# Placing the rows of matmul operands within 512 bytes in an encoder block on one Trainium2 core

## Chip, core and metric

The kernel runs on one core of one Trainium2 chip. The metric is the device time of one execution in microseconds (us). A difference between two kernels counts as one from about 0.5%.

## What is computed

One residual block for a stream of 2048 tokens of width 1024, in float32:

```
n  = rms_norm(x);  q|k|v|u|B|C|gate_attn|gate_conv = n @ W_in + b_in
A  = chunked attention, 8 heads of 64, each chunk of 64 sees itself and 8 before it
yB = B * dwconv3_causal(C * u)
h  = x + (sigmoid(gate_attn) * (A @ P_attn) + sigmoid(gate_conv) * (yB @ P_conv)) @ W_o
h += moe(rms_norm(h))            # 32 experts, 2 per token, w2(silu(x w1) * (x w3))
out = h + sigmoid(rms_norm(h) @ W_pg + b_pg) * (p @ W_pp)
```

## The kernel before

Nearly all the work is matmuls on TensorE. Every float32 operand is split into two parts, `hi` (a rounded copy, made by ScalarE, L79) and `lo` (the rest, a subtraction on VectorE or GpSimd, L80), and a product is made in three passes that add up in PSUM (`mm3`, L82 to L93: L90 hi x hi, L91, L92). In `matmul(ps, stationary, moving)` the stationary operand has 128 columns of 4 bytes, one row of 512 bytes per partition, and the moving one mostly 512 columns, 2048 bytes per partition. In the profile's names a matmul is written `acc<-moving,stationary`.

The stages follow each other, with some overlap:

- Stage 1 (to about 640 us): q, k, v of each tile of 128 tokens (`proj`: moving `wh`, `wl`; stationary `nh`, `nl`), scores (`KT` moving, `QT` stationary, L346), transposes of the probabilities (L378) and their product with the values (L391, L392).
- Stage 2 (to about 1650 us), in four blocks of 512 tokens: `conv` (three products of 24 matmuls for each of four groups of channels) and `gate` (two products of 24 matmuls, and then `proj_T(ch, ya)` and `proj_T(ch, yc, 4)` of 12 each, for each of eight groups) have the token operands `nh`, `nl`, `yh`, `yl`, `ych`, `ycl` moving and the weight chunks `whi`, `wlo` stationary; `out_proj` has the chunks moving and `mh`, `ml` stationary. Routing (L668 to L760) runs between them, and near its end the first halves of p @ W_pp (`plain`: `wpph`, `wppl` moving, `ph`, `pl` stationary).
- Stage 3 (to about 2465 us): 32 experts in an order by their token counts; 18 of them have room for 192 tokens (rows A of 128 and B of 64), the others for 128. `gemm1` multiplies `xAh`, `xAl` and `xB` (stationary) with chunks of w1 and w3, `gemm2` `aAh`, `aAl` and `aB` with chunks of w2. B is one stationary of hi and lo side by side, so it needs two passes (L1034, L1035).
- Stage 4: the last gate, `whi`, `wlo` and one resident chunk `w7h`, `w7l` moving, `xh`, `xl` stationary.

The weights come as a stream of chunks of 512 KB (`prefetch`, L451 to L466): SP's queue loads `wraw` (L458), the split makes `whi` and `wlo`, 7 buffers of each in stages 3 and 4, 4 in stage 2, and TensorE frees them.

The addresses of the tiles follow from the order and the sizes in which the pools hand them out: pools of the left side (`cst`, `s1att`, `s2left`, `s3two`, `s4two`) grow upwards, pools of `side="right"` (`keep`, `wstream`, `s2right`, `ppool`) downwards. A tile of an odd size moves all that come behind it.

Of the kernel before, what the change touches and what calls it, by code (L numbers as in the profile page):

```python
# [7 lines left out]
F32 = mybir.dt.float32  # L8
# [7 lines left out]
DRAM = bass.MemoryType.DRAM  # L16
# [8 lines left out]
NE = 32  # L25
CAP = 192
NBIG = 18
# [18 lines left out]
def triangle():  # L46
    """[p < j | 1]"""
    return np.concatenate([np.arange(128)[:, None] < np.arange(128)[None, :], np.ones((128, 128))], 1).astype(np.float32)


def constants():
    c = np.zeros((128, NCST), np.float32)
    put = lambda n, v: c.__setitem__((slice(None), slice(*CO[n])), v)
    put("iota", np.arange(CAP))
    put("i4", 4 - np.arange(4))
    put("i8", 8 - np.arange(8))
    put("p", np.arange(128)[:, None])
    # expert 0 comes first whatever its count
    key = NE - 1 - np.arange(NE) + (np.arange(NE) == 0) * 2.0 ** 20
    put("key", key)  # L60
    put("kcol", key[np.arange(128) % NE][:, None])
    put("eid", (np.arange(128) % NE)[:, None])
    return c


# relative position of query row i of a tile and key column j of its band of 640
# [7 lines left out]
class K:  # L74
# [7 lines left out]
    def mm3(self, ps, st, mv, i0, n):  # L82
        """ps += st.T @ mv in three passes; st, mv = lists of (hi, lo)"""
        k = len(st)
        for i in range(k):
            sh, sl = st[i]
            mh, ml = mv[i]
            first = (i0 + i == 0)
            last = (i0 + i == n - 1)
            self.nc.tensor.matmul(ps, sh, mh, start=first, stop=False)  # L90
            self.nc.tensor.matmul(ps, sh, ml, start=False, stop=False)  # L91
            mm = self.nc.tensor.matmul(ps, sl, mh, start=False, stop=last)  # L92
        return mm  # L93

    # ---------------------------------------------------------------- setup
# [17 lines left out]

    def bank(self, dt=F32):
        self.nbank += 1
        return self.banks[self.nbank % len(self.banks)].tile([128, 512], dt, name="acc")

    def rstd(self, out, ss, n, width=1):
        """out = (ss/n + eps) ** -0.5 on Pool"""
        nc = self.nc  # L120
        nc.gpsimd.tensor_scalar(out, ss, 1.0 / n, EPS, op0=ALU.mult, op1=ALU.add)
        return nc.gpsimd.tensor_tensor(out, out, self.mhalf[:, :width], op=ALU.pow)

    # ---------------------------------------------------------------- stage 1
    def stage1(self, outer, after, lead=11, lag=2):
        tc, nc, a = self.tc, self.nc, self.a
        with ExitStack() as ctx:
# [14 lines left out]
            # the places of what the attention needs later serve the first loads  # L142
# [49 lines left out]
            # ---- projections of one tile, in four pieces  # L192
# [134 lines left out]
            # ---- attention, a unit = one head of one query tile  # L327
# [80 lines left out]
            fill = None  # L408
# [23 lines left out]
    # ---------------------------------------------------------------- weights, as a stream of [128, 1024] chunks  # L432
    def open_keep(self, ctx):
        nc = self.nc
        self.cst = ctx.enter_context(self.tc.tile_pool(name="keep", bufs=1, side="right", reuse_waits="tile"))
        self.cs = self.cst.tile([128, NCST], F32, name="cs")
        nc.scalar.dma_start(self.cs, self.a["cst"])
        self.gple = self.cst.tile([128, 8], F32, name="gple")
        nc.scalar.dma_start(self.gple, self.a["g_ple"][0].rearrange("(k p) -> p k", p=128))
# [7 lines left out]
    def add_chunk(self, parts, lo_eng=None, scale=None):  # L447
        """parts: function that gives [(view of a raw [128, 1024] tile, DRAM AP)]"""
        self.wsrc.append((parts, lo_eng, scale))
# [15 lines left out]
    def split_scaled(self, raw, hi, lo, scale, eng=None):  # L465
        """hi + lo = raw, or raw * scale with scale [128, 1]"""  # L466
        nc = self.nc
        if scale is None:
            return self.split(raw, hi, lo, lo_eng=eng)
        nc.scalar.activation(hi, raw, AF.Copy, scale=scale)  # L470
        nc.vector.scalar_tensor_tensor(lo, raw, scale, hi.bitcast(F32), op0=ALU.mult, op1=ALU.subtract)

    def chunk(self, ahead=2):
        """hi and lo of the next chunk; issues the chunks up to that one + ahead"""
        i = self.wcur
        self.wcur += 1
        self.prefetch(i + ahead)
        return self.wdone.pop(i)

    # ---------------------------------------------------------------- stage 2  # L480
    def stage2(self, outer, inner):
        """a generator: what it gives before the attention is done needs only the right side and ps_acc"""
# [18 lines left out]
        # what routing keeps  # L501
# [10 lines left out]
        with ExitStack() as ctx:  # L512
# [4 lines left out]
            bT = one([128, 28], "bT")  # L517
            nc.scalar.dma_start(bT, a["b_in"][0, 1536:5120].rearrange("(c p) -> p c", p=128))
            cw = one([128, 3, 4], "cw")
            for j in range(3):  # L520
                nc.scalar.dma_start(cw[:, j], a["conv_w"][0, j].rearrange("(c p) -> p c", p=128))
            cb = one([128, 4], "cb")
# [4 lines left out]
            halo = one([128, 4, 2], "halo")  # L527
# [24 lines left out]
            def proj_T(ch, n, k0=0):  # L552
                """[128 channels, 512 tokens]"""
                ps = bank()
                K_ = len(n)
                st = [(ch[0][:, (k0 + k) * 128:(k0 + k + 1) * 128], ch[1][:, (k0 + k) * 128:(k0 + k + 1) * 128]) for k in range(K_)]
                self.mm3(ps, st, n, 0, K_)
                return ps

            def conv(b, c, n):  # L560
# [5 lines left out]
                z = rt.tile([128, 514], F32, name="z", bufs=1)  # L566
# [34 lines left out]
            def out_proj(b, m):  # L601
                """a generator of the four tiles of block b"""
# [42 lines left out]
            def tail1(b, j, h):  # L645
                """h and its norm to DRAM; the norm's factor"""
                t0 = 512 * b + 128 * j
                nc.sync.dma_start(self.H[t0:t0 + 128, :], h)
                n2 = two.tile([128, D], F32, name="n2", bufs=2)
                ss = two.tile([128, 1], F32, name="ss")  # L650
                self.squared = nc.scalar.activation(n2, h, AF.Square, accum_out=ss)
                r = two.tile([128, 1], F32, name="rr", bufs=4)
                self.rooted = self.rstd(r, ss, D)
                nc.vector.scalar_tensor_tensor(n2, h, r, gffn, op0=ALU.mult, op1=ALU.mult)
                nc.sync.dma_start(self.N2[t0:t0 + 128, :], n2)
                return h, r

            def tail2(j, hr, LG):
                """the router's logits of the normed rows: (h * g @ w) * r + b"""
# [13 lines left out]
            def route(b, LG):  # L673
                """a generator: up to the ranks' matmuls, up to the slots' matmuls, the rest"""
# [64 lines left out]
                pick = T("pick", [4, NE])  # L739
# [22 lines left out]
            # from here on the left side is free too  # L762
# [4 lines left out]
            gT = two.tile([128, 8, 1], F32, name="gT", bufs=1)  # L767
            nc.scalar.dma_start(gT[:, :, 0], a["g_ffn"][0].rearrange("(k p) -> p k", p=128))
            wr = two.tile([128, 8, 36], F32, name="wr", bufs=1)
# [3 lines left out]
            br = two.tile([128, 36], F32, name="br", bufs=1)  # L773
# [48 lines left out]
    # ---------------------------------------------------------------- experts in the order of their counts  # L822
    def sort(self, pool, bank):
        """position of each expert by its count (0 for expert 0); the tokens of each position, the rows their outputs go to"""
# [16 lines left out]
        # pm[(q, e), i] = (pos[e] == i) * (1 or 128)  # L841
# [20 lines left out]
        # a slot that no token fills writes a row that nobody reads  # L862
        cT = T("cT", [32, 128])
# [5 lines left out]
        # blocks of 128 that the experts' tokens past their room fill  # L869
# [22 lines left out]
    def overflow_rows(self, pool):  # L892
        """for the tokens past their expert's room: place in the blocks of 128 that follow; the expert of each block"""
# [29 lines left out]
        # expert of block i = number of ends <= i  # L923
# [27 lines left out]
    # ---------------------------------------------------------------- stage 3  # L951
    def stage3(self):
# [3 lines left out]
        # positions below NBIG have room for CAP tokens, the others for 128; the two kinds alternate  # L956
# [31 lines left out]
        with ExitStack() as ctx:  # L988
# [48 lines left out]
            def fold(out, ps):  # L1037
                """out = the two halves of a B product, added"""
# [4 lines left out]
            def gemm1(x, gb=None):  # L1043
                """with gb the first matrix meets the rows A, then the rows B"""
# [192 lines left out]
    # ---------------------------------------------------------------- p @ w_ple_proj  # L1237
# [11 lines left out]
    def pp_half(self, n):  # L1249
        """the next n halves of tiles of p @ w_ple_proj, to DRAM, behind the last marked matmul"""  # L1250
# [21 lines left out]
    def plain(self, t, pool, name, bufs, eng=None):  # L1272
        """128 rows of p @ w_ple_proj, a generator of its halves"""
# [14 lines left out]
    # ---------------------------------------------------------------- stage 4  # L1288
    def stage4(self, out):
        tc, nc, a = self.tc, self.nc, self.a  # L1290
        with ExitStack() as ctx:
# [57 lines left out]
            def finish(t, h, r, pgs, pp, cuts, last):  # L1349
                """h + sigmoid(h * g @ w * r + b) * pp"""  # L1350
# [22 lines left out]
            order.close()  # L1373
            add(todo[0], *ld[0][:2])
            xs = turn(ld[0][1])
            r = norm(*ld[0][:2])
            for i, t in enumerate(todo):
# [8 lines left out]
                # the last tile's second half comes in two parts, each stored when it is done  # L1386
# [53 lines left out]
```

## Time and profile before

| what | value |
|---|---|
| time of three runs | 2697.61, 2699.0, 2709.66 us (median 2699.0) |
| span of the profiled execution, first to last instruction | 2698.6 us (the profile gives no other time of it) |
| TensorE matmul busy | 2636.4 us, 98% |
| VectorE, ScalarE, GpSimd busy | 62%, 50%, 31% |
| bytes from and to HBM | 400.30 and 62.39 MB, 171 GB/s over the span |

A busy share is a mean over stages. Matmuls overlap in this profile, so the time that one takes from the stream is the distance between two starts, not the duration of one.

### The profile page before, as it was taken

Reading aid. Unit: us, or ns where it says so; the run is one execution under the profiler, and the core shown is the slowest. Engines: PE = TensorE matmul, PEld = TensorE weight load, DVE = VectorE, ACT = ScalarE, POOL = GpSimd, SP = SyncE. Lnnn points to the kernel's source line nnn. Section 1 sums busy time; section 2 is a strip of 40 time slices with the busy share of each in tenths; the row PEclk is TensorE's granted clock in tenths of the full one; section 3 lists DMA queues with packets and bytes.
Section 4 is the critical chain, followed back from the end, with each engine's and each line's share of the span. In section 5 each row is a group of like instructions: output and inputs, shape, how many; then the busy total and the mean of one; then the engine's idle time right before and its main releaser. Section 6 shows DMA issues by size and latency. Waiting matters only on the chain.

```text
span 2698.6 us, 36516 instructions
## 1 busy us (share of the span) xinstructions
PE 2636.4 (98%) x13313; PEld 2183.9 (81%) x13313; DVE 1672.3 (62%) x2399; ACT 1341.7 (50%) x2025; POOL 838.2 (31%) x681
## 2 busy tenths in 40 slices
PE   7999999999999999999999998999999999998999
PEld 6888888878888888888888886888888888887887
DVE  7788867775344444444545446677777778675654
ACT  5666665563233323332333224766666666665322
POOL 2665565510000100010001003544544545452222
PEclk9999999999999999999999998999999999999999
DMA  5221311054345334533453346888988889887653
GB/s 182 71 71 56 109 47 40 9 137 139 95 139 172 102 94 141 172 94 94 142 162 94 94 149 211 302 303 289 308 302 302 294 295 314 301 301 264 215 180 109
DMA packets 349624, 465.11 MB, mean 172 GB/s; under 512 B 26241, under 2 KB 222081, under 8 KB 349441
## 3 DMA queue, kind: packets, MB, share of 16 engines
q1 hardware_dynamic: 314944, 388.35, 44.3%
q0 software_dynamic: 12096, 43.00, 4.4%
q10 hardware_dynamic: 22400, 31.41, 3.5%
q8 instruction: 105, 1.72, 0.3%
q14 instruction: 79, 0.64, 0.1%
HBM read 400.30 MB, written 62.39 MB: 171 GB/s over the span
## 4 chain that ended last, share of the span: by engine, by line
PE 89%; DVE 5%; DMA 2%; issue 1%; ACT 1%; POOL 1%; another core or an unknown queue 0%; ACTq 0%; SPq 0%; DVEq 0%; POOLq 0%
PE acc L90 24%; PE acc L92 23%; PE acc L91 23%; PE acc L1034 4%; PE acc L1035 4%; PE big L346 2%; PE big L378 2%; PE acc L391 1%; PE acc L392 1%; PE acc L1003 1%; PE acc L670 1%; DMA wraw<-w 1%; PE acc L292 1%; DVE PTl L384 1%; PE acc L1084 0%
## 5 line engine op out<-in xcount | busy, mean ns | idle before, releaser
L80 DVE TENSOR_TENSOR wlo<-wraw,whi 128x1024 fp32r<-128x1024 f32 x464 | 690.4, 1499 | 506.8 <-ACT whi L79 495.4
L79 ACT CAST whi<-wraw 128x1024 fp32r<-128x1024 f32 x560 | 584.9, 1050 | 810.5 <-PE acc L91 388.5
L90 PE MATMUL acc<-nh,whi 128*128 128x512 f32 x896 | 355.1, 398 | 1.0 <-ACT nh L79 1.0
L91 PE MATMUL acc<-nl,whi 128*128 128x512 f32 x896 | 355.2, 396 | 0.0
L92 PE MATMUL acc<-nh,wlo 128*128 128x512 f32 x896 | 354.3, 395 | 0.0
L80 POOL TENSOR_TENSOR wlo<-wraw,whi 128x1024 fp32r<-128x1024 f32 x96 | 236.5, 2464 | 130.8 <-ACT whi L79 122.1
L595 POOL TENSOR_TENSOR sa<-sa,sc 128x512 f32<-128x512 f32 x32 | 41.4, 1294 | 553.2 <-DVE sc L594 506.9
L90 PE MATMUL acc<-whi,xAh 128*128 128x512 f32 x512 | 207.1, 404 | 0.0
L91 PE MATMUL acc<-wlo,xAh 128*128 128x512 f32 x512 | 203.0, 397 | 0.0
L92 PE MATMUL acc<-whi,xAl 128*128 128x512 f32 x512 | 202.9, 397 | 0.0
L90 PEld LDWEIGHTS acc<-nh,whi 128*128 128x128 f32 x896 | 168.2, 188 | 41.2 <-ACT nh L79 1.9
L92 PEld LDWEIGHTS acc<-nh,wlo 128*128 128x128 f32 x896 | 168.4, 188 | 39.8
L91 PEld LDWEIGHTS acc<-nl,whi 128*128 128x128 f32 x896 | 168.5, 188 | 38.5
L91 PE MATMUL acc<-wl,nh 128*128 128x256 f32 (+1 forms) x512 | 173.8, 340 | 3.3 <-DVE wl L80 3.3
L90 PE MATMUL acc<-wh,nh 128*128 128x512 f32 (+1 forms) x512 | 175.9, 344 | 0.0
L92 PE MATMUL acc<-wh,nl 128*128 128x256 f32 (+1 forms) x512 | 174.3, 341 | 0.0
L383 ACT CAST PTh<-big 128x640 fp32r<-128x640 f32 (+4 forms) x128 | 80.3, 628 | 83.8 <-PE big L378 82.8
L365 ACT ACTIVATE L<-L,mn 128x640 f32<-128x640 f32 (+4 forms) x128 | 98.4, 769 | 38.6 <-DVE mn L363 15.1
L92 PEld LDWEIGHTS acc<-whi,xAl 128*128 128x128 f32 x512 | 96.6, 189 | 23.6 <-DVE xAl L1007 0.2
L90 PEld LDWEIGHTS acc<-whi,xAh 128*128 128x128 f32 x512 | 96.7, 189 | 22.7 <-ACT xAh L1006 0.2
L1034 PE MATMUL acc<-whi,xB 128*128 128x512 f32 x288 | 114.5, 398 | 0.0
L91 PEld LDWEIGHTS acc<-wlo,xAh 128*128 128x128 f32 x512 | 96.9, 189 | 21.5
(328 smaller groups left out, 5944.1 us busy)
## 6 DMA issues: line engine op xcount, KB each, us to landing
wraw<-w SPq DMA_DIRECT2D x384, 512.0 KB
wraw<-w_in SPq DMA_DIRECT2D x112, 512.0 KB
wraw<-w_o SPq DMA_DIRECT2D x32, 512.0 KB
y<-Y SPq DMA_DIRECT2D x32, 512.0 KB
xt<-x SPq DMA_DIRECT2D x16, 512.0 KB
xt<-NTd SPq DMA_DIRECT2D x16, 512.0 KB
nraw<-NTd ACTq DMA_DIRECT2D x32, 256.0 KB
wraw<-w_pa SPq DMA_DIRECT2D x32, 256.0 KB
```

The lines of the kernel that those rows point to most:

```text
L79: (hi_eng or self.nc.scalar.copy)(hi, raw)
L80: (lo_eng or self.nc.vector).tensor_sub(lo, raw, hi.bitcast(F32))
L90: self.nc.tensor.matmul(ps, sh, mh, start=first, stop=False)
L91: self.nc.tensor.matmul(ps, sh, ml, start=False, stop=False)
L92: mm = self.nc.tensor.matmul(ps, sl, mh, start=False, stop=last)
L346: nc.tensor.matmul(big[:, 512 * c:512 * c + hi - lo], QT[g, t][:, s, h * 128:(h + 1) * 128], KT[0][:, h, ks:ks + hi - lo], start=(s == 0), ...
L365: nc.scalar.activation(L[:, :n], L[:, :n], AF.Exp, bias=mn, scale=-1.0, accum_out=sm)
L378: nc.tensor.transpose(pt[:, j * 128:(j + 1) * 128], L[:, j * 128:(j + 1) * 128], self.ident)
L383: nc.scalar.copy(hi, ptv)
L595: nc.gpsimd.tensor_tensor(sa, sa, sc, op=ALU.add)
L1034: nc.tensor.matmul(ps, st, ch[0][:, sl], start=first, stop=False)
L1035: nc.tensor.matmul(ps, st, ch[1][:, sl], start=False, stop=last)
```

## The change

It gives tiles of other sizes, so that what follows them lies elsewhere; it adds three tiles that nobody uses (`pad`), puts several small tiles in one (`small`, `misc`), and lets two small tiles take the place of others of the same size (`pick` that of `prod`, `cT` that of `rk`). The core of the diff (removed comments left out):

```diff
 def setup(self, ctx):
         self.banks, self.nbank = [], 0
+        c.tile([128, 88], F32, name="pad")
...
 def open_keep(self, ctx):
         nc.scalar.dma_start(self.cs, self.a["cst"])
+        self.cst.tile([128, 24], F32, name="pad")
...
 def stage2(self, outer, inner):
-            bT = one([128, 28], "bT")
+            small = one([128, 128], "small")
+            bT = small[:, 0:28]
-            cw = one([128, 3, 4], "cw")
+            cw = small[:, 28:40].rearrange("p (j c) -> p j c", j=3)
-            cb = one([128, 4], "cb")
+            cb = small[:, 40:44]
-            halo = one([128, 4, 2], "halo")
+            halo = small[:, 44:52].rearrange("p (c j) -> p c j", j=2)
...
-                z = rt.tile([128, 514], F32, name="z", bufs=1)
+                z = rt.tile([128, 640], F32, name="z", bufs=1)
...
-                pick = T("pick", [4, NE])
+                pick = T("prod", [4, NE])
...
-            gT = two.tile([128, 8, 1], F32, name="gT", bufs=1)
+            misc = two.tile([128, 448], F32, name="misc", bufs=1)
+            gT = misc[:, 0:8, None]
-            wr = two.tile([128, 8, 36], F32, name="wr", bufs=1)
+            wr = misc[:, 8:296].rearrange("p (k c) -> p k c", k=8)
-            br = two.tile([128, 36], F32, name="br", bufs=1)
+            br = misc[:, 296:332]
...
 def sort(self, pool, bank):
-        cT = T("cT", [32, 128])
+        cT = T("rk", [32, 128])
...
 def stage4(self, out):
             order.close()
+            two.tile([128, 48], F32, name="pad", bufs=1)
```

Every engine has the same instructions in the same order, but for the copy `cT` of `sort`, which VectorE now runs behind one small subtraction and not ahead of it. No wait is added. What changes is where operands begin. The table gives the first byte of each operand within a row of 512 bytes of its partition, and the distance from the moving rows to the stationary rows, modulo 512, both as the addresses of the two built programs have them:

```
matmuls                       before: moving, stationary, distance   after
stage 1  wh,wl / nh,nl        288  288    0                          288  288    0
         KT / QT              160 or 416  160   0 or 256             0 or 256  0   0 or 256
         PTh,PTl / Vt         160  160    0                            0    0    0
stage 2  nh,nl / whi,wlo       64   96   32                            0    0    0
         yh,yl / whi,wlo      480   96  128                          256    0  256
         ych,ycl / whi,wlo     96   96    0                            0    0    0
         whi,wlo / mh,ml       96  480  384                            0  256  256
         wpph,wppl / ph,pl     96   96    0                            0    0    0
stage 3  whi,wlo / xA,xB       96  160   64                            0    0    0
         whi,wlo / aA,aB       96  160   64                            0    0    0
stage 4  whi,wlo / xh,xl       96  160   64                            0  192  192
         w7h,w7l / xh,xl      160  160    0                            0  192  192
```

## Rows read from the trace of the kernel before

**Rows 1.** The page's first part: busy us (share of the span) x instructions.

```profile
PE 2636.4 (98%) x13313; PEld 2183.9 (81%) x13313; DVE 1672.3 (62%) x2399; ACT 1341.7 (50%) x2025; POOL 838.2 (31%) x681
```

**Rows 2.** The page's chain that ended last, shares of the span by engine.

```profile
PE 89%; DVE 5%; DMA 2%; issue 1%; ACT 1%; POOL 1%; another core or an unknown queue 0%; ACTq 0%; SPq 0%; DVEq 0%; POOLq 0%
```

**Rows 3.** Busy time in a stretch of stage 2 and one of stage 3.

```profile
core 0: us, PE busy (x) PEld busy (x) DVE busy (x) ACT busy (x) POOL busy (x), PEclk, DMA share, GB/s
1000.00:1300.00 300.00, 300.00 (x1358) 243.85 (x1357) 139.48 (x189) 102.34 (x130) 22.50 (x28) 1.00 0.39 123
1660.00:2340.00 680.00, 680.00 (x3185) 547.55 (x3184) 494.65 (x466) 448.71 (x561) 334.64 (x179) 1.00 0.87 297
```

**Rows 4.** Timeline, stage 2: start us, us, engine, line, operation, out<-moving,stationary; PEld loads weights.

```profile
1100.08 0.40 PE L90 MATMUL acc<-nh,whi 128*128 128x512 f32 x1
1100.08 0.19 PEld L91 LDWEIGHTS acc<-nl,whi 128*128 128x128 f32 x1
...
1100.31 0.40 PE L91 MATMUL acc<-nl,whi 128*128 128x512 f32 x1
```

**Rows 5.** Timeline of PE, stage 2: first and last of 48 matmuls, distance 32.

```profile
1089.59 0.40 PE L90 MATMUL acc<-nh,whi 128*128 128x512 f32 x1
...
1100.55 0.39 PE L92 MATMUL acc<-nh,wlo 128*128 128x512 f32 x1
```

**Rows 6.** Timeline of PE, stage 3: first and last of 65 matmuls, distance 64.

```profile
1781.65 0.40 PE L90 MATMUL acc<-whi,xAh 128*128 128x512 f32 x1
...
1796.58 0.39 PE L1035 MATMUL acc<-wlo,xB 128*128 128x512 f32 x1
```

**Rows 7.** Timeline of PE, stage 2, out_proj: first and last of 192 matmuls, distance 384.

```profile
787.21 0.40 PE L90 MATMUL acc<-whi,mh 128*128 128x512 f32 x1
...
831.60 0.40 PE L92 MATMUL acc<-whi,ml 128*128 128x512 f32 x1
```

**Rows 8.** Timeline of PE, one gate: 12 of y, 12 of yc, then nh.

```profile
681.17 0.39 PE L90 MATMUL acc<-yh,whi 128*128 128x512 f32 x1
...
683.98 0.39 PE L90 MATMUL acc<-ych,whi 128*128 128x512 f32 x1
...
685.36 0.39 PE L90 MATMUL acc<-ych,whi 128*128 128x512 f32 x1
...
686.72 0.40 PE L90 MATMUL acc<-nh,whi 128*128 128x512 f32 x1
```

**Rows 9.** Timeline of PE, p @ w: two of 24 matmuls at distance 0, 11 steps apart.

```profile
1620.90 0.39 PE L90 MATMUL acc<-wpph,ph 128*128 128x512 f32 x1
...
1623.39 0.39 PE L92 MATMUL acc<-wpph,pl 128*128 128x512 f32 x1
```

**Rows 10.** Groups of matmuls, forms apart: xcount | busy us, mean ns | idle before.

```profile
L90 PE MATMUL acc<-nh,whi 128*128 128x512 f32 x896 | 355.1, 398 | 1.0 <-ACT nh L79 1.0
...
L90 PE MATMUL acc<-whi,xAh 128*128 128x512 f32 x512 | 207.1, 404 | 0.0
...
L90 PE MATMUL acc<-whi,mh 128*128 128x512 f32 x256 | 101.3, 396 | 0.0
...
L90 PE MATMUL acc<-whi,xh 128*128 128x512 f32 x217 | 86.8, 401 | 0.4 <-ACT xh L1336 0.4
...
L90 PE MATMUL acc<-ych,whi 128*128 128x512 f32 x128 | 50.1, 392 | 0.0
...
L90 PE MATMUL acc<-w7h,xh 128*128 128x512 f32 x31 | 12.1, 389 | 0.0
```

**Rows 11.** Timeline of PE, stage 1: four score matmuls (one row), and what follows.

```profile
611.70 0.75 PE L346 MATMUL big<-KT,QT 128*128 128x320 f32 x4
612.29 0.28 PE L391 MATMUL acc<-PTh,Vt 128*128 128x256 f32 x1
```

**Rows 12.** The page's costliest groups: the split on DVE.

```profile
L80 DVE TENSOR_TENSOR wlo<-wraw,whi 128x1024 fp32r<-128x1024 f32 x464 | 690.4, 1499 | 506.8 <-ACT whi L79 495.4
```

**Rows 13.** Waits of SP's queue, the longest: us in total, times, longest us.

```profile
SPq L458 <- DVE wlo L80: 1100.2, 390, 7.6
```

## The prediction

> **What bounds the kernel now.** I read the page first, then the chain of waits, then busy time by stretches, then the forms of matmul, and last the timeline of TensorE (PE), where the change acts. PE is busy for 2636.4 of 2698.6 us [rows 1] and carries 89% of the chain that ended last [rows 2]; in the long stretches of stages 2 and 3 it is never idle (300 of 300 us, 680 of 680 us) at a granted clock of 1.00, the 2.4 GHz level [rows 3]. A change of a few ns for each matmul is therefore a change of the end, as long as operands keep arriving.
>
> How far apart two matmuls start is not the printed duration: with starts 0.23 us apart each row shows 0.40 us, because the matmuls overlap. I use differences of starts ("pitch") over long runs, so that the rounding to 0.01 us does no harm. 512 columns at 2.4 GHz are 213.3 ns. Beside each matmul the weight load of the next one runs: L91's load starts at 1100.08, with the matmul of L90, and its own matmul at 1100.31 [rows 4]. So the pair that reads on-chip memory (SBUF) at one time is the moving rows of one matmul and the stationary rows of the next, and their distance is what the change sets.
>
> The pitches by distance within a row of 512 bytes (table of the section on the change) are these:
> - distance 32 (nh, whi): 47 steps from 1089.59 to 1100.55, 233.2 ns [rows 5];
> - distance 64 (whi, xA): 64 steps from 1781.65 to 1796.58, 233.3 ns [rows 6];
> - distance 384 (whi, mh): 191 steps from 787.21 to 831.60, 232.4 ns [rows 7];
> - distance 128 (yh, whi): 12 steps from 681.17 to 683.98, 234.2 ns; and right behind it, same stage, same moving form, same whi, distance 0 (ych, whi): 12 steps to 686.72, 228.3 ns, of which the first six take 230.0 and the last six (from 685.36) 226.7 [rows 8];
> - distance 0 again (wpph, ph): 11 steps from 1620.90 to 1623.39, 226.4 ns [rows 9].
>
> So distance 0 settles some six matmuls after a disturbance at about 226.7 ns, 13.3 above the 213.3 of streaming; the others stay at 233.3, 20 above. That step of 6.6 ns is what the sum is made of. The mean durations agree: 398 for nh and 404 for xA, 392 for ych, 389 for w7h [rows 10].
>
> **The change, part by part.** No engine gets another instruction or another wait; the order stays, but for one DVE copy (below). Only addresses move. I take 227.0 ns for a matmul at distance 0 after the change: 226.7, and some 20 ns more (six matmuls at 230.0) after each break, spread over runs of 48 to 80.
>
> 1. Stage 2, nh and nl with whi and wlo, 32 to 0: 2688 matmuls (896 on each of three lines [rows 10]) x (233.2 - 227.0) = 16.7 us.
> 2. Stage 2, y with whi, 128 to 256, and yc with whi, which stays at 0 but begins at byte 0: 32 gate steps, each now 2.81 + 2.74 us [rows 8], then 24 x 0.227 = 5.45, so 0.10 each, 3.2 us. Distance 256 has one witness: four score matmuls of 320 columns start at 611.70 and the next form at 612.29, 147.5 ns each, 14 above their 133.3 [rows 11]; their moving rows begin at 160 and at 416 in turn, against 160, so half of them stand at 256 and all are as cheap as 0. Bounds: 128's price kept (0.5 us left, from yc) and that of 0 (3.2). I take the latter.
> 3. Stage 2, whi with m, 384 to 256: 768 matmuls (256 on each line [rows 10]) x (232.4 - 227.0) = 4.1 us; bounds 0 and 4.1, by the same witness.
> 4. Stage 3, whi with xA, xB, aA, aB, 64 to 0: xA 3 x 512 [rows 10]; the code gives 32 experts x 8 x 3 = 768 for aA, 18 x 16 x 2 = 576 for xB, 18 x 8 x 2 = 288 for aB; 3168 in all x 6.3 = 20.0 us.
> 5. Stage 4, whi with xh and xl, 64 to 192: 3 x 217 = 651 matmuls [rows 10]. No row shows 192. It lies between 128 (no gain) and 256 (6.3 ns, 4.1 us): I take the middle, 2.1 us. The 3 x 31 of w7 leave 0 for 192; now 389 where xh has 401 [rows 10], so the bounds are nothing and 93 x 6.3 = 0.6 us lost. I take nothing, since they never run more than three in a row.
> 6. At nothing: the score and P.V matmuls (distances stay 0 and 256), the projections of stage 1 (288 on both sides stays), transposes, the wider z, the scalars gathered in two tiles, and the shared names. The copy cT falls behind one small subtract on DVE while PE has other halves of p @ w to do; with that cover gone it costs less than the 1.5 us of a full split [rows 12].
>
> Sum: 16.7 + 3.2 + 4.1 + 20.0 + 2.1 = 46.1 us. The profiled execution's span is 2698.6; the page gives no time around it, and the median of the three runs is 2699.0, 0.4 more. I predict 2699.0 - 46.1, rounded to **2653 us**.
>
> Does all of it reach the end? Stage 3 is the place to ask: DMA's share is 0.87 at 297 GB/s [rows 3], and a pitch 2.7% shorter asks for about 0.89 and 305. But the queue that loads weights waits for buffers, not they for it: 390 waits on DVE's split, 1100.2 us in all [rows 13], and the split waits for buffers that PE frees. A faster PE shortens these waits first. Late next would be the weights of the experts with room for 128 tokens, which have the fewest matmuls for the same bytes, with a few us.
>
> **A rule that speaks against this.** The forecast stands on rows 5 to 9 alone. The Trainium skill (TensorE: Matmul & The Clock Gate, "Step-by-step: what each phase is for") says that PE has two independent SBUF read ports, one for the moving operand and one for the weight load, so that loading the next weights steals nothing from the running matmul. By that the sum would be 0 and the time 2699; by the rows it is 46. Rows 8 disagree with it: two kinds of run follow each other in one stage, alike in form, and differ by 6 to 7 ns a matmul.
>
> **The rivals.**
> - *It seldom settles.* Transposes and changes of operand break the runs, and the mean stays at 229.5 to 230, as in the first six of ych [rows 8]. Gain 3.5 ns x 7659 matmuls (the sum of 1 and 3 to 5, with 384 for y) = 27 us: **2672**. For it: many runs of 12 in stage 2. Against: most are 48 to 80 long, and neighbours get the same distance.
> - *A start at byte 0 gives a further step.* All distances that I can read are of rows that begin inside a row of 512. Moving rows of 2048 bytes that begin at 0 touch four such rows and not five. If that is worth one more step of 6.7 ns for the 8136 matmuls concerned (7659, and 477 of yc and w7), the gain is 46 + 54: **2599**. Nothing in the trace shows it; only that steps of this size exist speaks for it.
> - *Nothing changes* because distance is not the cause, but the place of a run or its operands: **2699**. Against it: 0 is cheap at two starting bytes (96 and 160), in two stages [rows 8 to 10].
> - *Slower.* With both rows at byte 0, weight load and matmul, which start together [rows 4], meet at the first byte, and each matmul pays one step more than today: 8136 x 6.7 = 54 us, **2753**. It decides from a mean pitch of 235 (1.7 ns above today's 233.3, 13.5 us in all). For it: no moving row of 512 columns begins at 0 today. Against: the pairs at 96 (yc, ph) meet at their first byte too, and are the cheapest.
>
> **How the numbers follow.** Forecast 0.62 (by itself 2640 to 2665, from the bounds of 2, 3 and 5 and a few us for late loads), seldom settles 0.13, a further step 0.12, nothing 0.08, slower 0.05. Leaving out the last two leaves out 0.13, so the range goes from just below the third case to just above the first rival: 2597 to 2684. About 0.5%, 13.5 us, is what a measurement here can tell from no change: the first three cases are faster by more (0.87), the fourth is within it (0.08), the last slower (0.05).
>
> **What would show it.** Right: runs of nh, xA and mh at 226.7 ns, their mean durations down from 396 to 404 to about 390; stage 3 some 20 us and stage 2 some 24 us shorter, stage 1 as it is; PE still never idle there. Wrong: runs of xA still at 233 (the cause is not distance), or at 220 (the start counts too); a pitch of 227 with new idle time before xA, released by DMA, would say that the loads became the bound.

## Result and profile after

Four runs of the changed kernel took 2658.07 to 2662.66 us, median **2661.45**; four of the kernel before had the median 2699.14. The ratio is 0.9846 (95% interval 0.9824 to 0.9868): 37.7 us faster, where 46.1 were forecast. In a later comparison of five rounds the same kernel had 0.9845 (0.983 to 0.986).

The profiled execution after spans 2659.4 us. First the page's first part, the answer to [rows 1]:

```profile
PE 2595.2 (98%) x13313; PEld 2184.5 (82%) x13313; DVE 1675.8 (63%) x2399; ACT 1341.6 (50%) x2025; POOL 841.0 (32%) x681
```

The same number of instructions; only PE's busy time fell, by 41.2 us. The chain that ended last, the answer to [rows 2]:

```profile
PE 84%; DVE 6%; DMA 4%; issue 3%; POOL 1%; ACT 1%; SPq 0%; another core or an unknown queue 0%; DVEq 0%; POOLq 0%; ACTq 0%
```

PE's share fell from 89 to 84% and DMA's rose from 2 to 4%: somewhere the chain left PE. Not in the long stretches, as the windows that answer to [rows 3] show (same columns):

```profile
1000.00:1300.00 300.00, 300.00 (x1389) 249.49 (x1388) 146.31 (x198) 105.92 (x135) 23.64 (x29) 1.00 0.41 132
1660.00:2340.00 680.00, 680.00 (x3256) 559.69 (x3256) 513.29 (x477) 461.98 (x578) 348.44 (x184) 1.00 0.89 307
```

PE is never idle there and does 1389 matmuls in 300 us where it did 1358, 3256 in 680 where it did 3185. Now the timeline of PE after. The rows for y, mh, nh and x (679.68 to 1088.88, 1755.90 and 1770.40) are the same matmuls as in [rows 5 to 8]; 568.62, 1629.37 and 2455.16 are the first matmuls of stages 2, 3 and 4, and 2654.60 is the last of the kernel:

```profile
568.62 0.50 PE L90 MATMUL acc<-nh,whi 128*128 128x512 f32 x1 [0.52 <-ACT nh L79]
...
679.68 0.39 PE L90 MATMUL acc<-yh,whi 128*128 128x512 f32 x1
...
682.40 0.39 PE L90 MATMUL acc<-ych,whi 128*128 128x512 f32 x1
...
685.12 0.39 PE L90 MATMUL acc<-nh,whi 128*128 128x512 f32 x1
...
783.04 0.39 PE L90 MATMUL acc<-whi,mh 128*128 128x512 f32 x1
...
826.33 0.39 PE L92 MATMUL acc<-whi,ml 128*128 128x512 f32 x1
...
1078.23 0.39 PE L90 MATMUL acc<-nh,whi 128*128 128x512 f32 x1
...
1088.88 0.39 PE L92 MATMUL acc<-nh,wlo 128*128 128x512 f32 x1
...
1629.37 0.79 PE L90 MATMUL acc<-whi,xAh 128*128 128x512 f32 x1
...
1755.90 0.39 PE L90 MATMUL acc<-whi,xAh 128*128 128x512 f32 x1
...
1770.40 0.39 PE L1040 MATMUL acc<-wlo,xB 128*128 128x512 f32 x1
...
2455.16 0.47 PE L90 MATMUL acc<-whi,xh 128*128 128x512 f32 x1
...
2499.89 0.40 PE L90 MATMUL acc<-whi,xh 128*128 128x512 f32 x1
...
2509.51 0.39 PE L90 MATMUL acc<-w7h,xh 128*128 128x512 f32 x1
...
2654.60 0.28 PE L92 MATMUL acc<-w7h,xl 128*128 128x256 f32 x1
```

The four marks between the stages in the trace before:

```profile
568.06 0.51 PE L90 MATMUL acc<-nh,whi 128*128 128x512 f32 x1
...
1652.45 0.80 PE L90 MATMUL acc<-whi,xAh 128*128 128x512 f32 x1
...
2493.48 0.48 PE L90 MATMUL acc<-whi,xh 128*128 128x512 f32 x1
...
2693.74 0.28 PE L92 MATMUL acc<-w7h,xl 128*128 128x256 f32 x1
```

Read off, pitch is the distance of two starts over the steps between them:

| run of matmuls | steps | pitch before, ns | after, ns |
|---|---|---|---|
| nh, whi (distance 32, now 0) | 47 | 233.2 [rows 5] | 10.65/47 = 226.6 |
| x (64, now 0) | 64 | 233.3 [rows 6] | 14.50/64 = 226.6 |
| mh (384, now 256) | 191 | 232.4 [rows 7] | 43.29/191 = 226.6 |
| y (128, now 256) | 12 | 234.2 [rows 8] | 2.72/12 = 226.7 |
| yc (0, now 0 behind y at 256) | 12 | 228.3 [rows 8] | 2.72/12 = 226.7 |
| xh (64, now 192), from 2499.89 | 42 | | 9.62/42 = 229.0 |

| stage, from mark to mark | before | after | difference | forecast |
|---|---|---|---|---|
| 1 | 568.06 | 568.62 | +0.6 | 0 |
| 2 | 1084.39 | 1060.75 | -23.6 | -24.0 |
| 3 | 841.03 | 825.79 | -15.2 | -20.0 |
| 4 | 200.26 | 199.44 | -0.8 | -2.1 |

Mean durations answer to [rows 10]:

```profile
L90 PE MATMUL acc<-nh,whi 128*128 128x512 f32 x896 | 349.7, 392 | 2.0 <-ACT nh L79 2.0
...
L90 PE MATMUL acc<-whi,xAh 128*128 128x512 f32 x512 | 204.1, 399 | 0.4 <-ACT xAh L1011 0.4
...
L90 PE MATMUL acc<-whi,mh 128*128 128x512 f32 x256 | 99.9, 390 | 0.0
...
L90 PE MATMUL acc<-whi,xh 128*128 128x512 f32 x217 | 86.2, 398 | 1.8 <-ACT xh L1341 1.8
```

nh fell from 398 to 392, mh from 396 to 390, xA from 404 to 399, xh only from 401 to 398.

What was waited for at the end of stage 3 (POOL's split `wlo`) and in stage 4 (the cast `xh`), PE's waits before:

```profile
PE acc L91 <- POOL wlo L80: 1.9, 1, 1.9
...
PE acc L90 <- ACT xh L1336: 0.4, 1, 0.4
```

and after (us in total, times, longest):

```profile
PE acc L91 <- POOL wlo L80: 2.6, 1, 2.6
...
PE acc L90 <- ACT xh L1341: 1.8, 1, 1.8
```

Both grew. The chain after (start, us, what) tells where the cast was late: in stage 4 it runs through the loads of H.

```profile
2580.42 6.87 DMA h<-H
2587.41 1.30 DVE h L1321
...
2593.67 0.70 DVE o L1363
2594.43 7.20 DMA h<-H
...
2607.97 0.70 DVE o L1363
2608.73 7.10 DMA h<-H
2615.95 1.29 DVE h L1321
2617.27 1.30 DVE h L1322
...
2619.79 0.48 ACT xh L1341
2620.32 0.51 PE acc L90
```

Each load starts right behind the add L1363, the last reader of the older `h`, and takes some 7 us; one round is 14.0 to 14.3 us (2580.42, 2594.43, 2608.73). In the chain of before this circle is there too, but only from 2634.47 on. How long it rules differs between executions of one kernel: the first load of H in the chain after starts at 2487.40, in that of the changed kernel's second profiled execution (beside the better placings, below) at 2578.87.

### The profile page after: what moved, and what is told of

Same layout as the page of the kernel before. It is cut to its first block, busy times and chain, and to the rows that moved or that the text cites. A ratio compares the mean times of both kernels' runs of the same rounds, so it can differ in the third digit from the quotient of the medians.

```text
span 2659.4 us, 36515 instructions
## 1 busy us (share of the span) xinstructions
PE 2595.2 (98%) x13313; PEld 2184.5 (82%) x13313; DVE 1675.8 (63%) x2399; ACT 1341.6 (50%) x2025; POOL 841.0 (32%) x681
## 4 chain that ended last, share of the span: by engine, by line
PE 84%; DVE 6%; DMA 4%; issue 3%; POOL 1%; ACT 1%; SPq 0%; another core or an unknown queue 0%; DVEq 0%; POOLq 0%; ACTq 0%
PE acc L90 22%; PE acc L92 22%; PE acc L91 22%; PE acc L1039 4%; PE acc L1040 4%; PE big L348 2%; PE big L380 2%; DMA h<-H 1%; DMA wraw<-w 1%; PE acc L393 1%; PE acc L394 1%; PE acc L1008 1%; PE acc L674 1%; PE acc L294 1%; POOL g L1362 1%
## 5 line engine op out<-in xcount | busy, mean ns | idle before, releaser
L90 PE MATMUL acc<-nh,whi 128*128 128x512 f32 x896 | 349.7, 392 | 2.0 <-ACT nh L79 2.0
L91 PE MATMUL acc<-nl,whi 128*128 128x512 f32 x896 | 350.0, 391 | 0.0
L92 PE MATMUL acc<-nh,wlo 128*128 128x512 f32 x896 | 348.8, 389 | 0.0
L90 PE MATMUL acc<-whi,xAh 128*128 128x512 f32 x512 | 204.1, 399 | 0.4 <-ACT xAh L1011 0.4
L91 PE MATMUL acc<-wlo,xAh 128*128 128x512 f32 x512 | 200.1, 391 | 0.0
L92 PE MATMUL acc<-whi,xAl 128*128 128x512 f32 x512 | 200.0, 391 | 0.0
L90 PEld LDWEIGHTS acc<-nh,whi 128*128 128x128 f32 x896 | 168.1, 188 | 37.2 <-ACT nh L79 2.7
L92 PEld LDWEIGHTS acc<-nh,wlo 128*128 128x128 f32 x896 | 168.3, 188 | 34.5
L91 PEld LDWEIGHTS acc<-nl,whi 128*128 128x128 f32 x896 | 168.3, 188 | 33.4
L90 PE MATMUL acc<-wh,nh 128*128 128x512 f32 (+1 forms) x512 | 176.6, 346 | 0.3 <-ACT wh L79 0.2
L91 PE MATMUL acc<-wl,nh 128*128 128x256 f32 (+1 forms) x512 | 174.1, 341 | 2.1 <-DVE wl L80 2.1
L92 PE MATMUL acc<-wh,nl 128*128 128x256 f32 (+1 forms) x512 | 174.5, 342 | 0.0
L90 PEld LDWEIGHTS acc<-whi,xAh 128*128 128x128 f32 x512 | 96.5, 189 | 20.8 <-ACT xAh L1011 1.0
L92 PEld LDWEIGHTS acc<-whi,xAl 128*128 128x128 f32 x512 | 96.3, 188 | 20.5 <-DVE xAl L1012 0.2
L1040 PE MATMUL acc<-wlo,xB 128*128 128x512 f32 x288 | 112.2, 390 | 0.0
```

What stands on the lines that cost most here:

```text
L1040: nc.tensor.matmul(ps, st, ch[1][:, sl], start=False, stop=last)
```

## The experiments

All edits are given against the changed kernel. "Undisturbed" steps below are differences between the starts of neighbouring matmuls of one operand (nh with nl, x with a, mh with ml and so on), without those more than 16% above the shortest, which hold a wait, a change of operand or half clock.

**Does the start byte or the distance count?** Every operand 96 bytes further, all distances as in the changed kernel:

```diff
-        c.tile([128, 88], F32, name="pad")
+        c.tile([128, 112], F32, name="pad")
...
-        self.cst.tile([128, 24], F32, name="pad")
```

> Every operand of the changed kernel begins 96 bytes later within its row of 512 (whi, nh, x at 96 instead of 0, m and y at 352, xh at 288); all distances stay. Distance decides: long runs of nh, xA, m stay at 226.7 ns a matmul and the time stays at 2661 us, within 0.3%. The start at byte 0 decides: the runs go back to 233 ns and the time to about 2699 us. Both count: something between, near 2680 us.

Measured: 2667.25 us over four runs, ratio 0.9863 (0.9843 to 0.9882) to the kernel before in the same comparison (2702.84). The 47 steps of nh, now with both rows at byte 96, in its timeline:

```profile
1080.88 0.39 PE L90 MATMUL acc<-nh,whi 128*128 128x512 f32 x1
...
1091.54 0.39 PE L92 MATMUL acc<-nh,wlo 128*128 128x512 f32 x1
```

10.66/47 = 226.8 ns. Undisturbed means: nh 227.1, x 227.4, m 226.9, y 226.7, all four as in the changed kernel. The start byte does not count: two rivals of the prediction fall with this, a further step for byte 0 and a collision at byte 0.

**Are the distances the whole of the change?** Their old values again (32, 128, 384, 64, 64), everything else as changed, `whi` at byte 0:

```diff
-                z = rt.tile([128, 640], F32, name="z", bufs=1)
+                z = rt.tile([128, 520], F32, name="z", bufs=1)
-            misc = two.tile([128, 448], F32, name="misc", bufs=1)
+            misc = two.tile([128, 480], F32, name="misc", bufs=1)
...
+            two.tile([128, 16], F32, name="pad")
...
-            two.tile([128, 48], F32, name="pad", bufs=1)
+            two.tile([128, 16], F32, name="pad", bufs=1)
```

> The distances of the kernel before, in the places of the changed one: whi still begins at byte 0 of a row, and moves there against m at 384, x at 64, xh at 64; nh begins at 480 (distance 32) and y at 384 (128). Distance decides: runs back to 233.2 (nh), 233.3 (x), 232.4 (m) and 234 (y) ns and the time back to about 2698 us. The start of the moving rows at byte 0 decides: runs of m, x, xh, whose moving rows still begin at 0, stay at 227 ns, only nh and y go back, and the time is about 2680 us.

Measured: 2701.34 us over ten runs, ratio 0.9997 (0.9987 to 1.0007) in the same comparison. The runs of nh and x in its timeline:

```profile
1091.06 0.40 PE L90 MATMUL acc<-nh,whi 128*128 128x512 f32 x1
...
1102.02 0.39 PE L92 MATMUL acc<-nh,wlo 128*128 128x512 f32 x1
...
1781.40 0.40 PE L90 MATMUL acc<-whi,xAh 128*128 128x512 f32 x1
...
1796.33 0.40 PE L1041 MATMUL acc<-wlo,xB 128*128 128x512 f32 x1
```

10.96/47 = 233.2 and 14.93/64 = 233.3, to the rounding the pitches of [rows 5, 6]. So the whole gain is that of the distances; the gathered scalars and shared names are worth nothing.

**Which distances are cheap?** Three kernels give each operand another distance. First x at 192, m, y and xh at 0:

```diff
-            small = one([128, 128], "small")
+            small = one([128, 64], "small")
-            misc = two.tile([128, 448], F32, name="misc", bufs=1)
+            misc = two.tile([128, 384], F32, name="misc", bufs=1)
...
+            two.tile([128, 48], F32, name="pad")
...
-            two.tile([128, 48], F32, name="pad", bufs=1)
```

> The changed kernel with three distances exchanged: stage 3 (x, a) at 192 instead of 0, m and y at 0 instead of 256, xh in stage 4 at 0 instead of 192. Distance decides: m and y stay at 226.7 ns (0 and 256 are alike), xh falls from 229 to 226.7 ns, and x rises to the 229 ns that xh had at 192; time about 2665 us (3168 x 2.3 ns more, 651 x 2.3 less). If each stage has a distance of its own that suits it: m and y go up, to 230 or more, and xh too, and the time to 2670 us or more.

One run: 2668.76 us. Its run of x, 64 steps:

```profile
1754.75 0.39 PE L90 MATMUL acc<-whi,xAh 128*128 128x512 f32 x1
...
1769.40 0.40 PE L1041 MATMUL acc<-wlo,xB 128*128 128x512 f32 x1
```

14.65/64 = 228.9 ns: 192 costs about a third of a step of 6.67 in stage 3 as well, and xh at 0 is at 227.1.

Second, nh 320, x 256, m 64, y 448, xh 256 (`z` 592, `misc` 528, and pads of 64 in stages 3 and 4):

> Four other distances: nh 320, stage 3 at 256, m at 64 and y at 448, xh at 256. Distance decides, with 0 and 256 alike: x, a and xh at 226.7 ns, m at 233.3 as x had at 64; nh at 320 and y at 448 have no row yet, near 233 if only 0 and 256 are cheap; time about 2661 + 2688 x 6.5 ns + 768 x 6.5 ns - 1.5 = 2682 us. If 256 was cheap for m and y alone, x goes to 233 and the time to some 2700 us.

One run: 2684.67 us. Its run of x:

```profile
1780.17 0.39 PE L90 MATMUL acc<-whi,xAh 128*128 128x512 f32 x1
...
1794.68 0.39 PE L1041 MATMUL acc<-wlo,xB 128*128 128x512 f32 x1
```

14.51/64 = 226.7 ns at 256, in the stage with the densest transfers. Third, nh 96, m 160, y 352, x 224, xh 96, and Vt of stage 1 64 bytes behind PTh and PTl (`z` 536, `misc` 424, pads of 56 and 24, 16 floats ahead of `Vt`):

> Distances that no run has shown yet: nh 96, m 160 (y 352), x 224, xh 96; and in stage 1 the values Vt at 64 instead of 0 behind the probabilities (256 columns a matmul). If only the distance modulo 256 counts, 96 should cost what 352 costs, and lie near the 233.3 ns of 32 and 64; 160 and 224 lie beside 128 (233) and 192 (229), so 228 to 233 ns. Vt: the last tile of the kernel before showed 113 ns at 64 and stage 1 shows 119 to 120 at 0; if distance counts for 256 columns too, 113 ns here, 672 x 6 ns = 4 us less in stage 1. Time: about 2661 + 2688 x 6.5 + 3168 x 0 to 6 + 768 x 0 to 6 = 2679 to 2705 us.

One run: 2702.26 us, beside 2699.55 for the kernel before.

The undisturbed means of one operand in one run, lowest and highest of all runs, for 512 moving columns:

| distance | modulo 256 | ns | measured on |
|---|---|---|---|
| 0, 256 | 0 | 226.7 to 227.4 | nh, x, y, yc, m, xh |
| 16 | 16 | 226.7 or 233.3 (mean 230.5) | xh |
| 32 | 32 | 233.2 | nh, x |
| 64, 320 | 64 | 233.3 to 233.4 | x, m, xh; nh |
| 96, 352 | 96 | 234.0 to 234.3 | nh, xh; y |
| 128, 384 | 128 | 232.4 to 232.8 | y; m |
| 160 | 160 | 233.4 (after L90 and L92 231.4, after L91 237.3) | m |
| 192, 448 | 192 | 229.0 to 229.7 | x, xh; y |
| 224 | 224 | 233.2 | x |

Left out is yc at 0 where the y just ahead of it has a dear distance: 228.1 to 229.2, with the first steps dearer, as in [rows 8]. The distance modulo 256 orders the rest, wherever the operands stand and whichever moves. But at two distances it does not settle the price alone. At 192 it is neither end: with xh after, three matmuls take 226, 229 and 232 ns in turn, yet in the last of the three profiled executions of the changed kernel two tiles of xh ran at 233.3. And at 16, in the run that comes next, no tile runs at the mean: a tile of xh has the cheap pitch or the dear one almost from its first matmul to its last, but for one tile that changes behind a break and one that holds a stretch at half clock. Two neighbouring tiles there, from the fourth matmul on:

```profile
2526.91 0.39 PE L90 MATMUL acc<-whi,xh 128*128 128x512 f32 x1
...
2535.75 0.39 PE L90 MATMUL acc<-whi,xh 128*128 128x512 f32 x1
...
2538.69 0.39 PE L90 MATMUL acc<-whi,xh 128*128 128x512 f32 x1
...
2547.09 0.39 PE L90 MATMUL acc<-whi,xh 128*128 128x512 f32 x1
```

8.84/39 = 226.7 and 8.40/36 = 233.3 ns at one distance in one kernel. What chooses between them is open.

**Which pair has to fit?** Only `ml` is moved by 64 bytes, to 320 from the weight chunks, `mh` stays at 256; with it x at 32 and xh at 16:

```diff
+                if b == 0 and c == 0:
+                    two.tile([128, 16], F32, name="mpad", bufs=1)
...
+            two.tile([128, 8], F32, name="pad")
...
-                hi = two.tile([128, 8, 128], F32R, name="xh")
+                hi = two.tile([128, 1152], F32R, name="xh")[:, 4:1028].rearrange("p (k c) -> p k c", k=8)
...
-            two.tile([128, 48], F32, name="pad", bufs=1)
```

(`b`, the number of the block, is handed to `gate`; `xl` as `xh`.)

> The tiles ml (stationary of the third pass only) moved 64 bytes on: whi moves against mh at 256 as before, and only the load of ml lies at 320 from the chunk that moves while it loads, which is wlo of the second pass. If the pair that counts is the moving rows of one matmul and the stationary rows of the next, the step behind the second pass (L91) grows and the other two keep 226.7 ns; if it is a matmul's own stationary, the step behind the third pass (L92) grows. In both cases the mean of the three rises by about a third of 6.6 ns, to some 229 ns. Beside it, x at 32 in stage 3 (233.3 ns if distance decides, as nh had at 32) and xh at 16 in stage 4 (unknown: 226.7 if only steps of 32 bytes or more count).

One run: 2678.16 us. Its run of m, 191 steps:

```profile
780.54 0.39 PE L90 MATMUL acc<-whi,mh 128*128 128x512 f32 x1
...
824.68 0.40 PE L92 MATMUL acc<-whi,ml 128*128 128x512 f32 x1
```

44.14/191 = 231.1 ns, where 229 was expected. From start to start, the steps that follow L90 (mh), L91 (mh) and L92 (ml) took 228.4, 229.2 and 235.6 ns on average, where the changed kernel has 226.9, 226.7 and 226.9. Most of it lies behind the matmul whose own weights were displaced, not beside the load of those weights, which runs with L91. That speaks against the prediction's picture of one pair (a matmul and the load of the next). But the three grew by 12.7 ns together, nearly two steps of 6.67 for one displaced operand in three; so more than one neighbour matters. Which, stays open. This is one run and one displacement; in every other run here all three operands have one distance, and the distance can be named without knowing the pair.

**A better placing.** xh and xl at 256, and Vt 64 bytes behind PTh and PTl, because 256 moving columns had taken 116.2 ns there and 119.0 at 0 (`small` is narrowed to make room):

```diff
+                if not V:
+                    att.tile([128, 16], F32, name="vpad", bufs=1)
...
-            small = one([128, 128], "small")
+            small = one([128, 64], "small")
...
-            two.tile([128, 48], F32, name="pad", bufs=1)
+            two.tile([128, 64], F32, name="pad", bufs=1)
```

> The changed kernel with the last two pairs of tiles put at other distances: xh and xl of stage 4 at 256 (modulo 512) from the row start of their weights' partner instead of 192, and Vt of stage 1 64 bytes behind PTh and PTl instead of 0. Theory (the step depends on the distance modulo 256; 0 is the good one for 512 columns, and 64 was the better one for 256 columns): xh and xl go from a mean of 229 to 226.9 ns, 651 x 2.3 = 1.5 us less; the 256-column steps of P.V from 119 to 116 ns, 672 x 3 = 2.0 us less; about 2658 us, 3.5 us below the changed kernel run beside it, hardly to be told apart by time, plainly by the steps. Rival (the distance modulo 512 counts): xh at 256 stays at 229 or above. Second rival: the steps shorten and the gain comes back as waits for H and for the transposed xh in stage 4, time equal to the changed kernel's within 1 us.

The second has 48 floats in `vpad` (Vt at 192) and no pad in stage 4 (xh at 0):

> As the run before, but xh and xl at 0 and Vt at 192. Theory: xh and xl 227.1 ns, 1.3 us less; P.V at 192 between the 119 of distance 0 and the 116 of distance 64, 118 expected, 0.7 us less; about 2659.5 us. Rival (192 is for 256 columns as dear as or dearer than 0): P.V 119 or more, about 2660.2 us.

and the changed kernel beside both:

> The changed kernel itself, beside the two. All theories: its steps as before (nh, x, m, y at 226.6 to 227.6 ns, xh at 229), 2661.5 us, 0.985 of the kernel before.

Five rounds each: 2659.16 us (ratio 0.9829, 0.9815 to 0.9844), 2659.49 (0.9832, 0.9817 to 0.9847), and 2660.47 (0.9845, 0.983 to 0.986) for the changed kernel. The steps came as expected (the 113 ns that the third sweep had expected for P.V at 64 did not come, it took 116 there too): xh 227.0 in both, P.V 116.0 to 116.7 at 64 and 117.3 to 117.8 at 192, against 229.0 and 119.0.

The times are 1.3 and 1.0 us lower, where the steps would give 3.5 and 2.0, and well inside the intervals: these rounds show no gain in time.

**Is part of the gain given back?** The undisturbed steps account for more than the difference of the times, so the rest must have grown, or differ by chance. Three more executions, two of the kernel before and one of the changed kernel, without an edit:

> The kernel before, unchanged, to see how much its own executions differ outside the undisturbed steps. So far, against its one profiled execution, stages 3 and 4 of the five executions with the changed distances spent 1.6 to 12.6 us more on disturbed steps (waits, half clock, changes of operand), and the one with the old distances 3.0 us less. Theory (the faster matmuls run into waits, so part of the gain comes back): this execution is within 3 us of the first one there, stages 3 and 4 together, and its matmul steps are the same to 0.1 ns (nh 233.3, x 233.3, m 232.4). Rival (only scatter between executions): it differs by 3 to 10 us, upwards as well.

> The kernel before once more, same expectations: theory within 3 us of its first execution in the disturbed steps of stages 3 and 4, rival 3 to 10 us away.

> The changed kernel once more. Undisturbed steps: stage 2 23.7 us, stage 3 17.6 us, stage 4 2.9 us less than in the kernel before, as in its two other executions (all theories). Disturbed steps of stages 3 and 4: theory 2 to 8 us more than in the kernel before; rival (scatter) anything from 5 less to 8 more.

The table compares each execution, matmul by matmul, with the first profiled one of the kernel before (us). Undisturbed means here both starts of 512-column neighbours less than 262 ns apart in both executions; the rest is all else between the marks.

| execution | stage 2 undisturbed, rest | stage 3 | stage 4 |
|---|---|---|---|
| changed, first | -23.7, +0.1 | -17.6, +2.4 | -2.9, +2.0 |
| changed, beside the better placings | -23.6, -0.8 | -17.7, +2.1 | -2.8, +4.3 |
| changed, last | -23.7, +1.7 | -17.6, +1.1 | -2.5, +5.5 |
| 96 bytes further | -23.6, +3.1 | -17.4, +5.2 | -2.9, +7.8 |
| xh 256, Vt 64 | -23.7, +0.9 | -17.5, +2.7 | -4.4, +2.0 |
| xh 0, Vt 192 | -23.7, +2.4 | -17.5, +0.1 | -4.3, +5.2 |
| distances of before | +0.1, +0.7 | 0.0, -2.6 | +0.2, -0.8 |
| before, second | 0.0, -0.5 | +0.1, -0.8 | 0.0, +0.4 |
| before, third | +0.1, -0.5 | +0.1, -1.1 | 0.0, -0.4 |

The undisturbed columns repeat to 0.4 us. The rest scatters, but in stage 4 the four executions with the old distances (the first is 0) lie between -0.8 and +0.4 and the six with new ones between +2.0 and +7.8; in stage 3 between -2.6 and 0 against +0.1 and +5.2. The last changed execution had 6.6 in both stages together, which fits giving back (2 to 8 expected) and scatter (-5 to 8) alike; the two of before had -0.4 and -1.5 (within 3), which speaks against scatter. The widest values of the table, those of 96 bytes further, come from the slowest of its four runs (2675.26 us). The sweeps, left out of the table, fall in line: where a stage keeps dear distances, its rest is like that of the kernel before (the third sweep -2.4 in stage 3 and -0.2 in stage 4, the run with `ml` moved -1.4 in stage 3), and where it has cheaper ones the rest is above (stages 3 and 4 of the first sweep +0.8 and +8.5, of the second +1.9 and +2.4). So giving back is real, and not only scatter.

## Why the prediction was right, and by how much

**The mechanism was right.** Distance set the pitch; 0 and 256 settled at 226.7 ns, as read from [rows 8, 9, 11]. The single witness for 256, the score matmuls, held for 512 columns in three stages. The 233.2 of nh, 233.3 of x and 232.4 of m came down to 226.6 to 226.7. Transients after a break are there, but short: the mean over stage 2's undisturbed steps went from 232.65 to 226.95, where 227.0 was taken.

**Terms 1 to 3 (stage 2), 24.0 us:** 23.7 in the undisturbed steps and 23.6 from mark to mark; that the rest adds nothing there is luck to some 2 us, as the table shows.

**Term 4 (stage 3), 20.0 us:** 17.6 in the undisturbed steps, 15.2 in all. 2985 of the 3168 steps are undisturbed in both traces, and they fell from 233.28 to 227.38, by 5.9 and not 6.3. The missing 183 steps (1.2 us) and 0.4 ns x 2985 (1.2) make up the difference of 2.4: the runs of an expert are broken more often than the 64 steps of [rows 6] show.

**Term 5 (stage 4), 2.1 us, the middle between two bounds:** that the middle came near is luck, since no row showed 192; it does lie between, at 229.0, and the undisturbed steps give 2.9 us. From mark to mark only 0.8 is left.

**The step that failed** is "Does all of it reach the end?". It asked stage 3 alone and put what comes late at nothing in the sum. In three executions of the changed kernel, against four with the old distances, the rest of stage 3 is 1.9 against -1.1 us and that of stage 4 4.0 against -0.2: 3.0 + 4.2 = 7.2 us given back, and 0.4 in stage 2. With 44.2 us from the undisturbed steps (23.7 + 17.6 + 2.9) that leaves 36.6, close to the 37.7 measured.

What is late at the end of stage 3 is what the prediction named, weights: the last expert, one with rows A alone, waits for POOL's `wlo`, 2.6 us in the three executions of the changed kernel, 1.9, 1.1 and 1.6 in the three of the kernel before. Behind that wait PE runs at half clock, and for longer than before, as the windows of before and after show (columns of [rows 3]):

```profile
2455.50:2458.90 3.40, 3.40 (x10) 2.62 (x9) 3.21 (x6) 3.13 (x6) 0.00 (x0) 0.50 0.90 324
...
2414.00:2420.80 6.80, 6.30 (x17) 4.61 (x18) 6.33 (x8) 3.77 (x6) 0.00 (x0) 0.50 0.87 277
```

Granted clock 0.50, the 1.2 GHz level, for 3.4 us in all three executions of the kernel before and for 6.8 in all three of the changed one. An estimate from these figures: 1.1 us of wait and half of 3.4 us, 1.7, make up most of the 3.0 that stage 3 gives back. The kernel with xh at 0 and Vt at 192 bears it out: it waited 1.5 us there, had 3.4 us of half clock, and its rest in stage 3 is +0.1.

In stage 4 it is not weights but H: the circle of load, add and release in the chain above takes 14.0 to 14.3 us for a tile of tokens where it rules. PE's work on one tile takes 11.87 us (from one group of transposes to the next, over most of the stage) where it took 12.05 before, so PE was already faster than that circle, and now uses up the tiles that lie ready a little sooner; then it waits for `xh`. The price of half clock can come behind such a wait too. In the changed kernel beside the better placings PE stood idle for 1.54 us before 2618.16, and its windows show the clock right after:

```profile
2620.00:2622.50 2.50, 2.50 (x7) 2.01 (x6) 1.35 (x2) 1.02 (x2) 0.32 (x1) 0.50 0.54 129
```

Granted clock 0.50 again, and matmuls 427 ns apart: the matmuls of that stretch cost 200 ns more each. The last changed execution has such a stretch as well, from 2612.3 to 2615.7, the first has none (1.00 from 2455 to 2659), which goes with their rests in stage 4: 4.3, 5.5 and 2.0. That the circle of H is the cause in stage 4 is read from the chain; no run here took it away.

**The rivals.** "Seldom settles" (2672): the pitch was against it, though the time came nearer to it than a pitch of 227 alone would say. "Byte 0 gives a further step" and "slower" fell with the run 96 bytes further. "Nothing changes" fell with the run at the old distances: the same tiles and names, another distance, 2701.34 against 2661.45 us. The Trainium skill (TensorE: Matmul & The Clock Gate, "Step-by-step: what each phase is for") has the loads of the next weights take nothing from the running matmul. For 512 columns of this type the time of the stream is not free of where the weights lie: 226.7 against 233.3 ns by placing alone. Which read is held up by which, no run shows.

## What to carry to other kernels

Where PE is busy without a gap and loads 128 columns of weights for every 512 moving ones, in 4-byte operands as here, look at the pitch of matmul starts by operand pair before anything else; two kinds of run in one stage that differ by a few ns are a lever, and padding one tile to make moving and stationary rows begin a multiple of 256 bytes apart cost no time here. Then add up the gain stage by stage and ask in each, the short last one too, what else was just in time: here that took back 7 of 44 us.

## What was not expected

- The period is 256 bytes, not the row of 512 that the change works with: 320 is as dear as 64 (233.3 and 233.4 ns), 256 as cheap as 0.
- The price is not smooth: 232 to 234 ns from 32 to 160, 229 at 192, 233.2 at 224, 226.7 again at 256. At 192 it comes as a cycle of 226, 229 and 232.
- One distance can have two prices: at 16 whole tiles ran at 226.7 and others at 233.3, and at 192 two tiles of one execution at 233.3. A mean over tiles hides this.
- With 256 moving columns another distance is better: P.V takes 116.3 ns at 64, 117.5 at 192 and 119.0 at 0. That need not hold elsewhere: the 256-column matmuls of the last tile took some 118 ns in the first execution of the changed kernel and 113 in the two others, at one distance.
- One displaced operand of three cost nearly two steps, 12.7 ns in three matmuls.
